# Turning queries and keys once, and swapping their halves by transfers inside SBUF, in a two-layer hybrid transformer block

## The chip, the cores and the metric

The kernel runs on one core of a Trainium2 chip. Five engines work beside one another, each with an instruction queue of its own that it takes in order: TensorE (PE: matmuls, and transposes, which are matmuls with an identity), VectorE (DVE), ScalarE (ACT), GpSimdE (POOL), and SyncE (SP), which here issues the transfers (DMA). Semaphores order them against one another. The metric is device time in microseconds (us), the median of several runs.

## What is computed

Two layers work on 512 latent tokens and 256 context tokens of width 1024, with heads of 64 elements. Layer 0 has two parallel groups of attention heads, windowed ones with a sink and dense ones, four query heads to a key head; layer 1 has differential attention, two score maps per head. Queries and keys are normed and rotated, and then:

```python
# layer 0, dense heads (the windowed ones add a mask and a sink)
s = jnp.einsum('bqhgd,bkhd->bhgqk', qb, k).astype(jnp.float32) * scale
p = _softmax(s, sink_b).astype(v.dtype)
return jnp.einsum('bhgqk,bkhd->bqhgd', p, v)
...
# layer 1
s = jnp.einsum('bqhad,bkhad->bhaqk', qb, k).astype(jnp.float32) * scale
p = jax.nn.softmax(s, axis=-1)
a = (p[:, :, 0] - lam * p[:, :, 1]).astype(v.dtype)
return jnp.einsum('bhqk,bkhe->bqhe', a, v)
```

Each layer ends in an output projection and a SwiGLU feed-forward block. Everything is in float32.

## The kernel before, in words

**Split operands.** Matmuls run on a reduced float32 format (F32R). An operand is split into a high part (the value rounded to that format, a ScalarE copy) and a low part (the value less the high part, a subtraction), and products are summed from the parts. A head has only 64 elements, so a score matmul, whose contraction takes 128 partitions, holds both parts of an operand at once: one part in partitions 0 to 63, the other in 64 to 127. All four products of parts are wanted: high by high, low by low, and the two crossed ones. So each score takes two matmuls into one accumulator.

**How the four products are made before.** In layer 0 the query is turned (transposed by TensorE into its working layout) as high above low. The key is turned twice: once as high above high, once as low above low. The first matmul gives both query parts times the key's high part, the second both times its low part. In layer 1 it is the other way round: the key is turned as high above low, and the query twice, as high above high and as low above low.

**Layer 0, from 60 to 385 us.** `in_proj0` (lines 505 to 546) projects one group of heads b (four query heads, one key, one value head) for six tiles of 128 tokens, context tiles 4 and 5 first, then 0 to 3. For each tile it empties the accumulator (`qkv`, line 520), norms and rotates (`rotate`), multiplies by the norm's factor (line 523), splits the queries (`qd`, lines 524 to 526) and the key (`kd`, 527 to 530; the key stands doubled in it), and puts two calls on a list: `turn_q` (four transposes into a PSUM tile `qpt`, one ScalarE copy of 512 columns into `qt`) and `turn_k` (two transposes into `kpt`, one copy of 256 columns into two rows of `kT`). `attend0` (from line 548) takes one tile of queries through scores (lines 573 to 581, four heads with two matmuls per stretch of keys), softmax, transposes of the probabilities (`ppt`) and the product with the values (`av`). While group b attends, group b + 1 is projected and turned between its steps. The last tile of each group is turned early in the next group's attention, but all that is left is turned before group 3 starts (line 1320): group 3 begins with a tile that needs all keys.

**Layer 1, from 975 to 1300 us.** `Proj1` projects head h for the six tiles. `finish` (lines 672 to 689) empties the accumulator `inps`, rotates and splits; its `transposes` (691 to 703), called some steps later from the list `late`, turns queries (four transposes into `qpt`, one copy of 512 columns into `qt`) and keys (two transposes into `kpt`, one copy of 256 columns into `kT`). Context tiles have no queries, so 32 of 48 calls turn queries. `attend1` (from line 706) makes the scores of one head and one query tile, two softmaxes, their difference, and the product with the values. The main loop (from line 1673) runs three half-tiles of projection beside each attention step, so projection is about a head and a half ahead.

**Weights.** Layer 1's weights come in units of two 128-row blocks: three SP loads into one of two raw buffers (line 365), a ScalarE cast to the high part (line 370), a GpSimdE subtraction to the low part (line 371, `wil`). A load waits until its raw buffer is free, and everything behind it on SP waits too. In layer 0 SP loads projection weights (line 491), modulation weights `modw` (line 177, 512 KB each, in the same raw buffers) and, near 301 us, the output projection's weights (line 771).

**What sets the order.** TensorE's order is that of the code, written by hand, in most of the kernel (`tc.manual_schedule` on PE: from line 1175 to 1214, and from the sixth attention step of layer 0 to the end). Layer 0's projection of group 0 and its first attention steps lie outside. The order on all other engines, SP among them, comes from a planner that goes by priorities (program order, mostly) and by its own estimate of when an instruction can start. Semaphores follow from the order.

Of the kernel before, what the change touches and what calls it, by code (L numbers as in the profile page):

```python
# [12 lines left out]
F32R = mybir.dt.float32r  # L13
# [6 lines left out]
P = 128  # L20
# [7 lines left out]
HD = 64  # L28
# [23 lines left out]
def bc(ap, pos, n):  # L52

    dims = [list(d) for d in ap.ap]
    return AP(ap.tensor, ap.offset, dims[:pos] + [[0, n]] + dims[pos:])
# [8 lines left out]
def backbone(es: ExitStack, tc: tile.TileContext, x, c, ctx, c_ctx, mod_w, mod_b, norm_mix_w, norm_ffn_w,  # L64
# [3 lines left out]
    nc = tc.nc  # L68
# [47 lines left out]
    def f32(ap):  # L116
        return ap.bitcast(F32)
# [383 lines left out]

    def tables0(j, tabs, wp):
        tabs[j] = rope_tables(wp, *((ev_qn_a[0], ev_kn_a[0]) if j == 0 else (ev_qn_b[0], ev_kn_b[0])))

    def in_proj0(b, ws, tabs, wp, st, later, begun={}):
# [5 lines left out]
        for t in CTX_FIRST:  # L511
# [15 lines left out]
            kd = wp.tile([P, 2, 2, HD], F32R, name="kd", tag="kd", bufs=2)  # L527
            kb = bc(y[:, 4, :], 1, 2)
            nc.scalar.copy(kd[:, 0], kb)
            nc.gpsimd.tensor_sub(kd[:, 1], kb, f32(kd[:, 0]))  # L530
# [9 lines left out]
            def turn_k(t=t, kd=kd):  # L540
                pk = tr_tile("kpt", [P, 2, P], F32R)
                for j in range(2):
                    nc.tensor.transpose(pk[:, j, :], kd[:, j].rearrange("p a d -> p (a d)"), identr)
                nc.scalar.copy(kT[:, :, t * P:(t + 1) * P], f32(pk))
# [3 lines left out]
    def attend0(b, t, state, o_t, sink, negsink, mp):  # L548

        qs, kT, vv = state  # L550
# [14 lines left out]
        if isA and nx and t < NTX - 1:  # L565
            masks.append((t + 1 - xt0, 1))
        P4 = mp.tile([P, 4, TOK], F32, name="Pt", tag="Pt", bufs=2)
# [89 lines left out]
    class Proj1:  # L657
# [14 lines left out]
        def finish(self, t, ps):  # L672
# [9 lines left out]
            if nq:  # L682
                qd = wp.tile([P, 2, 2, 2, HD], F32R, name="qd", tag="qd", bufs=3)
                yb = bc(y[:, 0:2], 2, 2)
                nc.scalar.copy(qd[:, 0], yb)
                nc.vector.tensor_sub(qd[:, 1], yb, f32(qd[:, 0]))
# [4 lines left out]
            def transposes():  # L691
                if nq:
                    pt = tr_tile("qpt", [P, 2, 2, P], F32R)
                    for j in range(2):
                        for a in range(2):
                            nc.tensor.transpose(pt[:, j, a, :], qd[:, j, a].rearrange("p a d -> p (a d)"), identr)
                    qt = self.qp.tile([P, 2, 2, P], F32R, name="qt", tag="qt", bufs=5)
                    nc.scalar.copy(qt, f32(pt))
                    qs[t] = qt
# [6 lines left out]
    def attend1(h, t, state, o_t, nlam, subln, mp):  # L706
# [3 lines left out]
        E = []  # L710
        for a in range(2):
# [1219 lines left out]
```

## Time and profile before

| | |
|---|---|
| median of 3 runs | 1695.23 us (1695.23 to 1698.65) |
| span of the profiled execution | 1695.6 us; no other time is given for it |
| granted TensorE clock | 0.992 |
| VectorE, ScalarE, GpSimdE busy | 1146.7, 937.0, 696.4 us |
| transposes that turn queries | 96 in layer 0, 128 in layer 1 |
| transposes that turn keys | 48 in layer 0, 96 in layer 1 |
| transfers issued by SP and ACT | 194.64 MB at a mean of 115 GB/s |

A row of the groups names the line, the engine, the operation, the tile written and those read, the shape and the count; behind the bar stands the time in which at least one of the group was running, then the mean length of one in ns; behind the second bar the idle time ahead of them and who ended it. A row of the waits gives the total in us, the number and the longest. A row of the timeline gives start and length in us. A row of the transfers gives their size and the median time from issue to landing.

### The profile page before, as it was taken

To read this page: it belongs to the slowest core of one execution; us is meant where nothing else is said; L and a number is where in the kernel's file an instruction comes from. 1 tells how busy PE (TensorE), PEld (TensorE's weight loads), DVE (VectorE), ACT (ScalarE), POOL (GpSimd) and SP (SyncE) were. 2 spreads that over 40 slices of the span, in tenths; PEclk is the share of its full clock that TensorE was granted. 3 is DMA by queue.
4 is the path that set the end of the run, shared out by engine and by line. 5 is a ranking of instruction groups with operands and counts; after the bars stand their busy time and mean duration, and the time that the engine had idled before them with its cause. 6 is when DMAs were issued, how large, how long until landed. Compare 5 with 4: busy or idle time off the path is not lost. (4 is left out here: it accounts for less than half of the span.)

```text
span 1695.6 us, 28585 instructions
## 1 busy us (share of the span) xinstructions
PE 1631.5 (96%) x10390; PEld 1468.6 (87%) x10390; DVE 1146.7 (68%) x2014; ACT 937.0 (55%) x2011; POOL 696.4 (41%) x867
## 2 busy tenths in 40 slices
PE   6999999899999999999999989999999999999998
PEld 3977787677999999998777889999988899999887
DVE  3765656754799887767767656666666598887434
ACT  5565555745456665545554456666666555555320
POOL 2665554321346554412413366666664242221000
PEclk8999999999999999999999999999999999999999
DMA  9222221411455555439966311111112433331431
GB/s 319 69 71 74 70 70 50 164 60 38 129 167 172 164 159 162 134 108 347 296 184 189 99 43 38 48 42 44 50 45 97 125 93 102 111 101 57 137 99 62
DMA packets 218108, 194.64 MB, mean 115 GB/s; under 512 B 20016, under 2 KB 202864, under 8 KB 217968
## 3 DMA queue, kind: packets, MB, share of 16 engines
q1 hardware_dynamic: 217616, 192.62, 36.8%
q8 instruction: 81, 1.33, 0.3%
q14 instruction: 59, 0.48, 0.1%
q10 hardware_dynamic: 352, 0.21, 0.0%
HBM read 179.92 MB, written 12.87 MB: 114 GB/s over the span
## 5 line engine op out<-in xcount | busy, mean ns | idle before, releaser
L901 ACT CAST wbh<-wr 128x512 fp32r<-128x512 f32 x170 | 104.9, 621 | 130.2 <-PE p L933 73.4
L933 PE MATMUL p<-hT,wbh 128*128 128x256 f32 (+1 forms) x752 | 154.5, 299 | 0.0
L465 PE MATMUL inps<-wih,hT 128*128 128x384 f32 x512 | 144.2, 344 | 7.3 <-ACT qkv L677 7.3
L911 POOL TENSOR_TENSOR wbl<-wr,wbh 128x512 fp32r<-128x512 f32 x43 | 60.0, 1396 | 173.6 <-ACT wbh L901 173.6
L933 PEld LDWEIGHTS p<-hT,wbh 128*128 128x128 f32 x752 | 121.9, 191 | 0.2
L911 DVE TENSOR_TENSOR wbl<-wr,wbh 128x512 fp32r<-128x512 f32 x127 | 107.7, 858 | 21.0 <-ACT wbh L901 16.8
L933 PE MATMUL p<-hT,wbl 128*128 128x256 f32 (+1 forms) x376 | 111.9, 298 | 0.0
L933 PE MATMUL p<-t,wbh 128*128 128x384 f32 (+1 forms) x480 | 111.3, 318 | 0.0
L604 POOL TENSOR_SCALAR Pt<-Pt,rc 128x256 f32<-128x256 f32 (+3 forms) x96 | 74.6, 788 | 89.3 <-DVE rc L601 83.1
L231 POOL TENSOR_TENSOR modp<-modp 128x512 f32<-128x512 f32 x40 | 57.4, 1436 | 114.3 <-ACT modp L230 114.3
L465 PEld LDWEIGHTS inps<-wih,hT 128*128 128x128 f32 x512 | 93.3, 188 | 10.6 <-ACT qkv L677 9.7
L933 PE MATMUL p<-hTt,wbh 128*128 128x256 f32 (+1 forms) x480 | 101.0, 302 | 0.0
L887 POOL TENSOR_TENSOR wr<-wr 128x512 f32<-128x512 f32 x40 | 61.6, 1540 | 89.8 <-DVE ws L892 85.8
L933 PE MATMUL p<-b,wbh 128*128 128x384 f32 x368 | 93.8, 336 | 0.2 <-DVE c L961 0.2
L901 ACT CAST wbh<-ws 128x512 fp32r<-128x512 f32 x120 | 69.4, 579 | 43.1 <-PE p L933 29.0
L224 DVE SCALAR_TENSOR_TENSOR ma<-modw,cols,ma 128x256 f32<-128x256 f32 x140 | 89.2, 637 | 2.3
L592 ACT ACTIVATE Pt<-sc,nm 128x256 f32<-128x256 f32 (+3 forms) x96 | 67.6, 707 | 35.3 <-DVE nm L588 16.9
L465 PE MATMUL inps<-wil,hT 128*128 128x384 f32 x256 | 86.0, 336 | 0.0
L933 PEld LDWEIGHTS p<-t,wbh 128*128 128x128 f32 x480 | 82.9, 189 | 0.0
L911 DVE TENSOR_TENSOR wbl<-ws,wbh 128x512 fp32r<-128x512 f32 x120 | 81.7, 681 | 1.7 <-ACT wbh L901 1.6
L933 PEld LDWEIGHTS p<-hTt,wbh 128*128 128x128 f32 x480 | 78.3, 191 | 3.1 <-ACT modp L230 1.6
L230 ACT ACTIVATE modp<-modw,cols 128x256 f32<-128x256 f32 x160 | 68.4, 500 | 18.0 <-POOL ma L236 10.1
(355 smaller groups left out, 5217.9 us busy)
## 6 DMA issues: line engine op xcount, KB each, us to landing
modw<-in_mod_w_dram SPq DMA_DIRECT2D x96, 512.0 KB, 5.2
wr<-in_ffn_w_in_dram SPq DMA_DIRECT2D x176, 256.0 KB, 2.9
wdr<-in_ffn_w_out_dram SPq DMA_DIRECT2D x66, 512.0 KB, 3.7
wir<-in_od_w_in_dram SPq DMA_DIRECT2D x96, 128.0 KB, 2.3
hidm<-hid SPq DMA_DIRECT2D x44, 192.0 KB, 1.9
hr<-hidm SPq DMA_DIRECT2D x22, 192.0 KB, 3.5
x<-in_x_dram SPq DMA_DIRECT2D x8, 512.0 KB, 3.5
wir<-in_ev_w_in_dram SPq DMA_DIRECT2D x16, 256.0 KB, 3.5
```

What stands on the lines that cost most here:

```text
L224: nc.vector.scalar_tensor_tensor(acc, w[:, k], scale[k], acc, ALU.mult, ALU.add)
L230: nc.scalar.activation(pr[:, k], w[:, k], AF.Copy, scale=scale[k])
L231: nc.gpsimd.tensor_add(pr[:, 0:2], pr[:, 0:2], pr[:, 2:4])
L465: nc.tensor.matmul(ps, hs[j][:, k, :], ws[k // 2][z][:, k % 2, c0:c1], start=(k, j, z) == (0, 0, 0), stop=(k, j, z) == (KT - 1, 1, 0))
L592: turn["exp"] = nc.scalar.activation(p[:, :n], s, AF.Exp, bias=nm[:, c1], accum_out=sm[:, c1])
L604: nc.gpsimd.tensor_scalar(p[:, :n], p[:, :n], rc[:, hh:hh + 1], 1.0, ALU.mult, ALU.mult)
L887: nc.gpsimd.tensor_sub(w, raw[f, "G1"], w)
L901: nc.scalar.copy(hi, w)
L911: (nc.gpsimd if name == "G2" else nc.vector).tensor_sub(lo, raw[need[n]], f32(hi))
L933: nc.tensor.matmul(ps, w[:, k, :], H[b][h][:, k, :], start=first and k == 0 and q == 0, stop=final and k == 3 and q == 2, skip_group_check ...
```

## The change

Each operand that was turned twice is now turned once, as high above low. A second copy with the halves exchanged, low above high, is made from it by two transfers from SBUF to SBUF, one for each half of the partitions, issued by SP. Scores then come from (high above low) by (high above low) and (high above low) by (low above high); the four products are the same.

In layer 0 this concerns the keys (24 tiles: four groups, six tiles): one transpose and not two, a copy of 128 columns and not 256, and a split of 64 columns and not 128. Each transfer moves 64 partitions of 512 bytes. In layer 1 it concerns the queries (32 tiles: eight heads, four tiles): two transposes and not four, a copy of 256 columns and not 512, and a split of 128 columns and not 256 on ScalarE and on VectorE. Each transfer moves 64 partitions of 1024 bytes. Scores have as many matmuls as before.

`halves_swapped` puts a swap on a list and issues all but the newest; the newest is issued with the next one or, by `swapped()`, when the next attention step is begun in the code. In the code's order each swap so stands ahead of the scores that read it.

```diff
@@ -499,6 +499,18 @@
+    swaps = []
+
+    def swapped(left=0):
+        while len(swaps) > left:
+            to, src = swaps.pop(0)
+            for j in range(2):
+                nc.sync.dma_start(f32(to[HD * (1 - j):HD * (2 - j)]), f32(src[HD * j:HD * (j + 1)]))
+
+    def halves_swapped(to, src):
+        swaps.append((to, src))
+        swapped(1)
+
@@ -524,10 +536,9 @@
-            kd = wp.tile([P, 2, 2, HD], F32R, name="kd", tag="kd", bufs=2)
-            kb = bc(y[:, 4, :], 1, 2)
-            nc.scalar.copy(kd[:, 0], kb)
-            nc.gpsimd.tensor_sub(kd[:, 1], kb, f32(kd[:, 0]))
+            kd = wp.tile([P, 2, HD], F32R, name="kd", tag="kd", bufs=2)
+            nc.scalar.copy(kd[:, 0], y[:, 4])
+            nc.gpsimd.tensor_sub(kd[:, 1], y[:, 4], f32(kd[:, 0]))
@@ -538,10 +549,11 @@
-                pk = tr_tile("kpt", [P, 2, P], F32R)
-                for j in range(2):
-                    nc.tensor.transpose(pk[:, j, :], kd[:, j].rearrange("p a d -> p (a d)"), identr)
-                nc.scalar.copy(kT[:, :, t * P:(t + 1) * P], f32(pk))
+                pk = tr_tile("kpt", [P, P], F32R)
+                nc.tensor.transpose(pk, kd.rearrange("p a d -> p (a d)"), identr)
+                cs = slice(t * P, (t + 1) * P)
+                nc.scalar.copy(kT[:, 0, cs], f32(pk))
+                halves_swapped(kT[:, 1, cs], kT[:, 0, cs])
@@ -564,6 +576,7 @@
+        swapped()
         P4 = mp.tile([P, 4, TOK], F32, name="Pt", tag="Pt", bufs=2)
@@ -680,22 +693,21 @@
-                qd = wp.tile([P, 2, 2, 2, HD], F32R, name="qd", tag="qd", bufs=3)
-                yb = bc(y[:, 0:2], 2, 2)
-                nc.scalar.copy(qd[:, 0], yb)
-                nc.vector.tensor_sub(qd[:, 1], yb, f32(qd[:, 0]))
+                qd = wp.tile([P, 2, 2, HD], F32R, name="qd", tag="qd", bufs=3)
+                nc.scalar.copy(qd[:, :, 0, :], y[:, 0:2])
+                nc.vector.tensor_sub(qd[:, :, 1, :], y[:, 0:2], f32(qd[:, :, 0, :]))
...
-                    pt = tr_tile("qpt", [P, 2, 2, P], F32R)
-                    for j in range(2):
-                        for a in range(2):
-                            nc.tensor.transpose(pt[:, j, a, :], qd[:, j, a].rearrange("p a d -> p (a d)"), identr)
+                    pt = tr_tile("qpt", [P, 2, P], F32R)
+                    for a in range(2):
+                        nc.tensor.transpose(pt[:, a, :], qd[:, a].rearrange("p a d -> p (a d)"), identr)
                     qt = self.qp.tile([P, 2, 2, P], F32R, name="qt", tag="qt", bufs=5)
-                    nc.scalar.copy(qt, f32(pt))
+                    nc.scalar.copy(qt[:, 0], f32(pt))
+                    halves_swapped(qt[:, 1], qt[:, 0])
                     qs[t] = qt
@@ -708,6 +720,7 @@
+        swapped()
         for a in range(2):
             sc = p_sc.pool.tile([P, 1024], F32, name="sc", tag="sc", bufs=2)
```

## The prediction

> **What bounds the kernel now.** I read the page's totals first, then a table of two stretches, then the groups of instructions, then the waits, the transfers, and the timeline around the places that the change touches.
>
> ```profile
> PE 1631.5 (96%) x10390; PEld 1468.6 (87%) x10390; DVE 1146.7 (68%) x2014; ACT 937.0 (55%) x2011; POOL 696.4 (41%) x867
> ```
>
> TensorE is busy for 96% of the span and no other engine for more than 68%. An average over stages proves little, so the second view cuts out the two stretches that hold every edited line: layer 0's attention (60 to 385 us) and layer 1's (975 to 1300 us). Columns: length, then busy time per engine with its instructions, the granted clock, the share of the transfer engines, GB/s.
>
> ```profile
> 60.00:385.00 325.00, 304.30 (x2166) 246.45 (x2165) 201.66 (x459) 192.34 (x478) 162.18 (x248) 0.99 0.24 78
> 975.00:1300.00 325.00, 308.72 (x2133) 292.72 (x2132) 207.46 (x413) 212.09 (x539) 214.94 (x340) 0.99 0.18 51
> ```
>
> TensorE is the bound in both: 304.3 and 308.7 of 325 us, the others at most 215. Its clock is 0.99, so nothing is to be had there. What TensorE no longer does comes off the end, unless a new wait takes its place; its idle time, 20.7 and 16.3 us, is all that a lighter ScalarE or GpSimdE could give beyond that.
>
> **The change part by part.** Layer 1's queries: 32 tiles go from four transposes to two. Layer 0's keys: 24 tiles go from two to one. The groups (all of the run; busy time is after the bar, then the mean of one in ns):
>
> ```profile
> L696 PE MATMUL qpt<-identr,qd 128*128 128x128 f32 x128 | 16.9, 254 | 0.9 <-ACT qt L698 0.8
> ...
> L702 PE MATMUL kpt<-identr,kd 128*128 128x128 f32 x96 | 16.0, 249 | 1.7 <-POOL kd L689 1.6
> ...
> L535 PE MATMUL qpt<-identr,qd 128*128 128x128 f32 x96 | 11.7, 245 | 0.8 <-ACT qt L537 0.6
> ...
> L543 PE MATMUL kpt<-identr,kd 128*128 128x128 f32 x48 | 7.6, 237 | 0.7 <-ACT kT L544 0.6
> ```
>
> The mean is useless here, since transposes overlap; the busy time of a group of four against a group of two tells what two more cost. Layer 1: 16.9/32 = 528 ns against 16.0/48 = 333 ns, so two are worth 195 ns, and 32 tiles 6.2 us. Layer 0: 11.7/24 = 488 against 7.6/24 = 317, so one is worth 85 ns, and 24 tiles 2.0 us. The busy time holds part of the last transpose's tail, which doesn't go with the count; I take 5.6 and 2.0, together 7.6 us off TensorE's path, between 8.2 and, with as much taken off once more, 7.0.
>
> The evictions and splits shrink with them:
>
> ```profile
> L698 ACT CAST qt<-qpt 128x512 fp32r<-128x512 f32 x32 | 18.7, 586 | 2.7 <-PE qpt L696 2.6
> ...
> L703 ACT CAST kT<-kpt 128x256 fp32r<-128x256 f32 x48 | 18.2, 378 | 1.2 <-PE kpt L702 1.2
> ...
> L688 ACT CAST kd<-qy 128x128 fp32r<-128x128 f32 x48 | 14.3, 299 | 15.0 <-POOL qy L680 14.8
> ...
> L685 ACT CAST qd<-qy 128x256 fp32r<-128x256 f32 x32 | 13.0, 406 | 23.4 <-POOL qy L680 23.4
> ```
>
> In layer 1 each qt copy goes from the 512-wide row to the size of the 256-wide one (586 to 378 ns) and each qd cast from the 256-wide to the 128-wide (406 to 299): 0.31 us of ScalarE per tile, 10 us in all, beside TensorE's work. VectorE's qd difference, and in layer 0 the kd pair and the kT copy, shrink on engines that are idle over a third of the time; I cost them at nothing, and TensorE's busy stream is what hides them. Does ScalarE's relief reach TensorE? TensorE's largest wait in the second stretch is this (us in total, times, longest):
>
> ```profile
> PE inps L465 <- ACT qkv L677: 7.7, 10, 1.4
> ```
>
> That wait is the accumulator being emptied. Where a transpose group stood between the last projection and the next, it covered part of it, and that cover gets thinner by 0.17 us: 10 waits could grow by 1.7 us. A ScalarE with 5% less to do could shorten them by about as much, or by 2 us at best. I take 0.5 us of gain, between -2 and +1.7.
>
> What is added: two transfers within SBUF per tile, 112 in all, all issued by SP. No transfer of this kind is in the trace. The nearest rows, with the time from issue to landing, and SP's time for one issue (min/median/max):
>
> ```profile
> modw<-in_mod_w_dram SPq DMA_DIRECT2D x96, 512.0 KB, 5.2
> ...
> wir<-in_od_w_in_dram SPq DMA_DIRECT2D x96, 128.0 KB, 2.3
> ...
> out_dram<-x SPq DMA_DIRECT2D x2, 128.0 KB, 1.7
> L365 SPq DMA_DIRECT2D wir<-in_od_w_in_dram x42: 367/469/1345, 1020.0 to 1143.7; - x42
> ```
>
> A transfer of 32 KB (keys) or 64 KB (queries) should land some 1.7 to 2.3 us after its issue, if nothing is ahead of it; a pair takes SP about 0.9 us. So a swapped operand is there 2.6 to 3.2 us after its copy. Where its reader comes later than that, it costs nothing. [...]
>
> Layer 1's lead is long. Timeline, start and duration:
>
> ```profile
> 1019.67 0.59 ACT L698 CAST qt<-qpt 128x512 fp32r<-128x512 f32 x1
> 1029.41 0.59 ACT L698 CAST qt<-qpt 128x512 fp32r<-128x512 f32 x1
> 1040.53 0.35 PE L715 MATMUL sc<-kT,qt 128*128 128x256 f32 x1
> 1040.72 0.28 PE L716 MATMUL sc<-kT,qt 128*128 128x256 f32 x1
> 1040.84 0.40 PE L715 MATMUL sc<-kT,qt 128*128 128x512 f32 x1
> 1041.08 0.39 PE L716 MATMUL sc<-kT,qt 128*128 128x512 f32 x1
> 1059.59 0.37 SPq L365 DMA_DIRECT2D wir<-in_od_w_in_dram  x1
> 1061.97 0.35 PE L715 MATMUL sc<-kT,qt 128*128 128x256 f32 x1
> ```
>
> The query tile copied at 1019.67 is used at 1040.53, the one of 1029.41 at 1061.97: 20 us and more, against 3.2 needed. Behind a swap that waits for its copy, SP has only the weight loads of the next head; the code holds one swap back, so that its copy is mostly done when it is issued. A load that is held up by one pair is late by 0.9 us; the loads that a projection needs soon come two groups a head, so 7 heads could lose up to 7 x 0.9 = 6 us if nothing else covered it. I take 0.3, since the weight split of a load issued at 1020 is used several us later; the range keeps 0 to 6. The wait that each first use of a swapped tile adds to TensorE is one more among waits that the scores carry already; the score group that begins here waits for a bank and two operands and its matmuls still follow one another at the pace of the stream:
>
> ```profile
> 1111.07 0.28 PE L715 MATMUL sc<-kT,qt 128*128 128x256 f32 x1
> 1111.19 0.28 PE L716 MATMUL sc<-kT,qt 128*128 128x256 f32 x1
> ```
>
> 0.12 us apart, so 56 such waits cost 0 to 0.08 us each (0.08 is what the pair at 1040.53, 0.19 apart, takes more): 0.2 us taken, 4.5 at most.
>
> Layer 0 has one exposed place. The last head group's first scores, at 300 us, read all keys right after the last of them was turned:
>
> ```profile
> 299.20 0.33 PE L543 MATMUL kpt<-identr,kd 128*128 128x128 f32 x2
> 299.88 0.38 ACT L544 CAST kT<-kpt 128x256 fp32r<-128x256 f32 x1
> 300.16 0.92 SPq L177 DMA_DIRECT2D modw<-in_mod_w_dram  x2
> 300.46 0.98 PE L578 MATMUL sc<-kT,qt 128*128 128x256 f32 x4
> 301.13 0.49 SPq L771 DMA_DIRECT2D wor<-in_ev_w_out_dram  x1
> ```
>
> The four score matmuls are spaced like the four at 1040.53 (0.19, 0.12, 0.24 us), so the one that reads the swapped half of the last key tile starts at 300.46 + 0.55 = 301.0. The copy ends at 300.26. At best the pair is issued at once: 300.26 + 0.9 + 1.9 = 303.1, a stall of 2.1 us. At worst it goes out after the two 512 KB modw loads and lands behind them: 301.1 + 0.9 + 5.2 = 307.2, a stall of 6.2. Behind the stalled matmul stands everything that TensorE has, as its order is written by hand there; VectorE's row maximum, and through it ScalarE, wait for it. I take 3.5, nearer the lower end, since SP may well send the pair between the two loads. The first scores of all follow their key copy as closely:
>
> ```profile
> 76.77 0.36 ACT L544 CAST kT<-kpt 128x256 fp32r<-128x256 f32 x1
> 77.39 0.70 PE L578 MATMUL sc<-kT,qt 128*128 128x256 f32 x4
> 77.94 0.33 PE L465 MATMUL inps<-wihi,hTc 128*128 128x384 f32 x1
> ```
>
> There the planner orders TensorE and has projections to put ahead, as the third line shows; I take 0.5 us, between 0 and 2.6.
>
> **Sum.** -5.6 - 2.0 - 0.5 + 0.3 + 0.2 + 3.5 + 0.5 = -3.6 us. The profiled execution's span is 1695.6 us, 0.4 above the median of 1695.2, so the forecast of 1692.0 for such a span is 1691.6 as a median.
>
> **The rivals.** First, the saving is given back in layer 0: the pair at 300 us lands behind both modw loads (+6.2 instead of 3.5), and the thinner cover in front of the accumulator's emptying costs 1.7 instead of gaining 0.5. That gives 1691.6 + 2.7 + 2.2 = 1696.5 at its worst, 1694.5 with half. For it: the loads' issue at 300.16 is earlier than the copy's end, and every transfer of SP goes through one queue. [...] Against it: SP's order comes from a planner that sees the pair as ready before the second load.
>
> Second, slower: swaps stand on SP behind a weight load that is being held. SP's own waits show the hold (us in total, times, longest):
>
> ```profile
> SPq L365 <- POOL rs_q L159: 162.0, 7, 29.4
> ```
>
> Seven times, once a head, SP stands at a load until a raw buffer is free; the load at 1059.59 ends one. If the swap of the third query tile (copied at 1029.41) were queued behind such a load, it would go out after that unit's three issues, at 1059.59 + 3 x 0.47 = 1061.0, and land at 1061.0 + 0.9 + 2.3 = 1064.2. Its matmul would start, 0.19 after 1061.97, at 1062.2: 2.0 us of stall, 14 us over seven heads, 1705. It decides as soon as the pair is issued later than 1059; before the hold it has 30 us. Earlier tiles can't be behind it, as the load itself waits for work that follows their scores. Against it: the copy is done 30 us before the hold ends.
>
> Third, more gain: the pair at 300 us goes out at once (stall 2.1), ScalarE's relief gives its 2 us: 1691.6 - 1.4 - 1.5 = 1688.7.
>
> **How the numbers follow.** A measurement of this kernel can tell about 0.2%, 3.4 us, from no change: faster means below 1691.8, slower above 1698.6. The forecast case has 0.48 (1689 to 1694; its middle lies at the border: 0.28 below, 0.20 within), the first rival 0.24 (0.18 within, 0.06 slower, if held-up loads and first-use waits come to their upper ends as well), the held swaps 0.12 (slower), more gain 0.16 (faster). So faster 0.44, same 0.38, slower 0.18. The forecast's own range is 1689 to 1694; for eight in ten it reaches down to the third rival with the larger transpose saving, 1685, and up through the first rival to 1700, which leaves out the held swaps and little else.
>
> **What would show it.** In the profile after: L696's successor with 64 and L543's with 24 transposes, qt copies near 380 ns; TensorE's busy time in the second stretch lower by 5 to 6 us and in the first by 2; one idle gap of 2 to 6 us ahead of the scores near 300 us, released by a transfer; no TensorE wait for a transfer in layer 1. The prediction is wrong if scores of layer 1 wait for swapped queries, if weight splits release projections more often than now, or if TensorE's idle time in the second stretch grows by as much as its busy time falls.

## The result, and the profile after

The changed kernel takes 1708.9 us (median of 6 runs, 1707.8 to 1710.7) beside 1695.2 us for the kernel before (6 runs beside them): a ratio of 1.0080, 95% interval 1.0068 to 1.0091. It is slower by 13.6 us, and outside the range of 1685 to 1700. The profiled execution's span is 1707.5 us, 11.9 above that of before, and it is this difference that is placed below. In every run that has both, the time is 1.7 to 2.1 us above the span, so the profiled execution of before stands for some 1697.4 us, 2 us above its median: the traces show somewhat less of the loss than the medians do.

The edit did on the engines what it says. First the page's totals after, then three groups of instructions (columns: the count, min/median/max in ns, first and last start in us), then the two kinds of transfer it added (size, median us from issue to landing).

```profile
PE 1629.1 (95%) x10302; PEld 1462.9 (86%) x10302; DVE 1149.9 (67%) x2014; ACT 923.9 (54%) x2011; POOL 694.6 (41%) x867
```

```profile
L707 PE MATMUL qpt<-identr,qd x64: 222/231/305, 997.0 to 1280.8; 128*128 128x128 f32 x64
L709 ACT CAST qt<-qpt x32: 364/367/380, 998.4 to 1281.1; 128x256 fp32r<-128x256 f32 x32
...
L553 PE MATMUL kpt<-identr,kd x24: 220/221/281, 68.3 to 301.8; 128*128 128x128 f32 x24
```

```profile
qt<-qt SPq DMA_DIRECT2D x64, 64.0 KB, 2.7
kT<-kT SPq DMA_DIRECT2D x48, 32.0 KB, 1.9
```

There are 88 transposes fewer, the copies are as short as forecast (367 ns for 378), and the key transfers land in 1.9 us, within the 1.7 to 2.3 us that were taken; the query transfers took 2.7 us, above them (few landings are recorded, seven of 64 here). The two stretches of the prediction, after (length, busy time by engine, clock, transfer share, GB/s):

```profile
60.00:385.00 325.00, 297.93 (x2091) 239.60 (x2090) 195.94 (x447) 182.37 (x463) 155.16 (x240) 0.98 0.26 80
975.00:1300.00 325.00, 301.18 (x2045) 285.85 (x2046) 211.98 (x408) 196.75 (x531) 215.81 (x341) 0.99 0.23 65
```

TensorE is busy for 6.4 and 7.5 us less in 325 us. Part of that is only that the work comes later: the stretches lack 75 and 88 matmuls where 24 and 64 transposes were taken out. Over the whole span TensorE's busy time falls by 2.4 us and its idle time grows by 14.3, from 64.1 to 78.4. Matching the same matmuls in both traces tells where. The start of a matmul after, minus its start before:

| place | after minus before | in this stage |
|---|---|---|
| 122 us, start of layer 0's attention | +5.9 | +5.9 |
| 290 us, end of the third head group | +2.8 | -3.1 |
| 311 us, layer 0's fourth head group has begun | +8.5 | +5.7 |
| 975 us, end of layer 0's feed-forward | +9.0 | +0.5 |
| end | +11.9 | +2.9 |

Three stages lose clearly and one gains. The gain, and the sizes of the first and the last loss, are not what the sum had. The first 62 us, which hold no edited line, came out 1.4 us shorter after, so the edited part of the first stage lost 7.3 us. Counted so, the stages add up to 13.3, near the 13.6 of the medians. One pair of traces is a rough measure, though: in six other traces the edited lines lie behind 840 us, and they reach that point between 2.4 us ahead of this execution of before and 0.3 behind it.

**Around 300 us.** First TensorE's longest wait for a transfer, then stretches of 3 us, before and after.

```profile
PE sc L591 <- DMA kT<-kT: 3.3, 1, 3.3
```

```profile
304.00:307.00 3.00, 2.50 (x18) 1.93 (x17) 2.55 (x5) 2.42 (x6) 0.78 (x1) 1.00 1.00 345
307.00:310.00 3.00, 3.00 (x29) 1.73 (x26) 1.22 (x3) 1.48 (x4) 2.24 (x4) 1.00 1.01 396
```

```profile
304.00:307.00 3.00, 0.03 (x1) 0.06 (x1) 0.00 (x0) 0.00 (x0) 0.00 (x0) 0.80 0.82 250
307.00:310.00 3.00, 3.00 (x14) 2.90 (x15) 1.19 (x3) 0.63 (x2) 0.00 (x0) 0.50 1.03 392
310.00:313.00 3.00, 3.00 (x15) 2.70 (x15) 1.65 (x2) 1.49 (x4) 0.00 (x0) 0.56 1.03 421
```

Before, no stretch is idle. After, the scores wait 3.3 us for the last key tile's swap; then the granted clock is 0.50 for 6.8 us, and 14 matmuls go where 29 went. The wait costs 3.1 us and the low clock 2.6.

**In layer 1.** TensorE's waits for a weight's low part, between 975 and 1300 us, before and then after:

```profile
PE inps L465 <- POOL wil L371: 1.0, 1, 1.0
```

```profile
PE inps L465 <- POOL wil L371: 7.6, 6, 1.5
PE inps L465 <- ACT qkv L690: 7.5, 12, 1.5
```

The second line of after was 7.7 before: ScalarE's relief changed nothing there. The first grew by 6.6 us. The same place in one head, SP's timeline and then GpSimdE's and ScalarE's, before:

```profile
1019.99 3.60 SPq L365 DMA_DIRECT2D wir<-in_od_w_in_dram  x6
```

```profile
1020.32 1.84 POOL L371 TENSOR_TENSOR wil<-wir,wih 128x768 fp32r<-128x768 f32 x1
1024.98 1.84 POOL L371 TENSOR_TENSOR wil<-wir,wih 128x768 fp32r<-128x768 f32 x1
```

and after:

```profile
1028.63 0.38 SPq L365 DMA_DIRECT2D wir<-in_od_w_in_dram  x1
1029.10 1.11 SPq L508 DMA_DIRECT2D qt<-qt  x2
1030.26 1.11 SPq L365 DMA_DIRECT2D wir<-in_od_w_in_dram  x2
1031.47 1.11 SPq L508 DMA_DIRECT2D qt<-qt  x2
1032.68 1.58 SPq L365 DMA_DIRECT2D wir<-in_od_w_in_dram  x3
```

```profile
1033.67 0.83 ACT L370 CAST wih<-wir 128x768 fp32r<-128x768 f32 x1 [1.87 <-DMA wir<-in_od_w_in_dram]
```

```profile
1034.58 1.82 POOL L371 TENSOR_TENSOR wil<-wir,wih 128x768 fp32r<-128x768 f32 x1 [0.91 <-ACT wih L370]
```

A unit of a weight is three loads. Before, the third unit's loads go out as soon as its buffer is free (1019.99), and its low part is done 6.8 us later, just when TensorE needs it (1026.8). After, the buffer is free at 1028.6, but a pair stands between the first load and the other two, so that the unit is complete 1.1 us later and its low part is ready 7.8 us after the buffer, at 1036.4. TensorE had stood idle for 1.4 us by then.

### The profile page after: what moved, and what is told of

It reads as the page before. It is cut to its first block, busy times and chain, and to the rows that moved or that the text cites. A ratio compares the mean times of both kernels' runs of the same rounds, so it can differ in the third digit from the quotient of the medians.

```text
span 1707.5 us, 28652 instructions
## 1 busy us (share of the span) xinstructions
PE 1629.1 (95%) x10302; PEld 1462.9 (86%) x10302; DVE 1149.9 (67%) x2014; ACT 923.9 (54%) x2011; POOL 694.6 (41%) x867
```

## The experiments

The theory: the loss has three places (the start of layer 0's attention, the hand-over at 300 us, the swap pairs between layer 1's loads), and each can be mended by itself. The rivals: the planner's new order as a whole, or transposes that are worth nothing. Ratios are to the kernel before, run beside each kernel. A head of layer 1 is the time between the first projection matmuls of successive heads in the trace, the median of six. Head groups of layer 0 are counted from 1.

| kernel | ratio, 95% interval | median us | head, us |
|---|---|---|---|
| before | | 1693.1 to 1695.2 | 39.7 |
| after | 1.0080 (1.0068 to 1.0091) | 1708.9 | 40.0 |
| keys only | 1.0068 (1.0053 to 1.0083) | 1706.1 | 39.75 |
| queries only | 1.0032 (1.0018 to 1.0046) | 1698.9 | 39.9 |
| all, ScalarE's queue | 1.0233 (1.0215 to 1.0250) | 1734.3 | 44.0 |
| all, queries behind loads | 1.0091 (1.0074 to 1.0109) | 1709.0 | 40.1 |
| keys, group 1 | 1.0035 (1.0022 to 1.0047) | 1700.2 | |
| keys, groups 2 and 3 | 0.9986 (0.9975 to 0.9996) | 1692.0 | |
| keys, group 4 | 1.0023 (1.0012 to 1.0033) | 1698.9 | |
| group 4, wait filled | 1.0041 (1.0027 to 1.0054) | 1700.6 | |
| group 1, x tiles only | 1.0019 (1.0009 to 1.0030) | 1698.0 | |
| group 1, no transfer | 0.9998 (0.9987 to 1.0009) | 1695.1 | |
| queries, loads first | 0.9994 (0.9981 to 1.0007) | 1693.3 | 39.15 |
| queries, no transfer | 1.0014 (1.0005 to 1.0023) | 1695.5 | 39.8 |
| queries, no transfer, loads first | 1.0016 (1.0007 to 1.0024) | 1697.5 | 39.8 |
| before, loads first | 1.0009 (0.9998 to 1.0020) | 1696.9 | 39.7 |
| queries, loads first, exp ahead | 1.0022 (1.0012 to 1.0033) | 1698.5 | 40.0 |
| all, loads first | 1.0062 (1.0048 to 1.0077) | 1706.0 | 39.1 |
| combined | 0.9984 (0.9973 to 0.9995) | 1691.3 | 39.2 |
| combined, queries as before | 1.0003 (0.9993 to 1.0012) | 1694.6 | 39.75 |

**Each half by itself.** Keys only: layer 1 as before.

```diff
-                    pt = tr_tile("qpt", [P, 2, P], F32R)
...
+                    pt = tr_tile("qpt", [P, 2, 2, P], F32R)
...
-                    halves_swapped(qt[:, 1], qt[:, 0])
```

> Layer 0's keys are swapped by transfers as in the changed kernel; layer 1's queries are turned twice on TensorE as before. Theory (three places each lose something: the start of layer 0's attention, the last score tile before 300 us with the clock after it, and layer 1's weight groups held up on SP): the loss of layer 0 stays whole and layer 1 gives back nothing and loses nothing, so the span is 8 to 9 us above the kernel before, some 1703 to 1705, with a TensorE wait of about 3 us for a transfer into kT near 300 us. Rival (the order that the planner wrote down has changed throughout, and the loss is in no one place): the span lies anywhere from 1692 to 1709 and the wait near 300 us need not be there.

Measured: 11.5 us above before, more than expected. In the traces the same matmuls are late by 6.7 us at 120 us, by 4.2 at 200 and by 8.9 after 305, and layer 1's heads take what they took before. Queries only: layer 0 as before.

```diff
-                pk = tr_tile("kpt", [P, P], F32R)
...
-                halves_swapped(kT[:, 1, cs], kT[:, 0, cs])
+                pk = tr_tile("kpt", [P, 2, P], F32R)
```

> Layer 1's queries are swapped by transfers; layer 0's keys are turned twice on TensorE as before. Theory (the swap pairs stand on SP between the weight loads that a projection needs): up to 975 us every matmul stands where it stood before, and each head of layer 1 waits 1.0 to 1.5 us for a weight split, which eats the 0.7 us of its transposes: 2 to 4 us above the kernel before, 1697 to 1699. Rival (layer 1's loss in the changed kernel came from the shift that layer 0 handed on to it, not from the swaps): no waits for weight splits beyond those of before, and about 5.5 us below it, 1690.

Measured: 5.4 us above before, with 7.0 us of waits for low parts. So layer 1 loses without anything handed on from layer 0; that rival is out. The halves add to 16.9 us, the whole change is 13.6; the intervals allow that difference.

**Another queue, another place.** The swaps from ScalarE's queue:

```diff
-                nc.sync.dma_start(f32(to[...]), f32(src[...]))
+                nc.scalar.dma_start(f32(to[...]), f32(src[...]))
```

> The whole change, with the swaps issued from ScalarE's queue and not from SP's. Theory (SP's order is what costs): the waits of TensorE for weight splits in layer 1 go back to what they were before, and layer 1 ends 4 to 6 us earlier relative to its start than before; the transfer that the scores near 300 us wait for no longer stands behind a held weight load on SP, so that wait is at most 3 us as it was or shorter. ScalarE issues 112 transfers more, at about half a microsecond each, 56 us beside 924 busy. In sum 1697 to 1703. Rival (layer 1 loses because every transfer beside the loads slows them, whatever queue issues it): the waits for weight splits stay at 1.0 to 1.5 us a head and the time stays at 1707 to 1711.

TensorE's waits in layer 1 with the swaps on ScalarE's queue:

```profile
PE inps L465 <- POOL wil L371: 16.3, 6, 2.7
PE inps L465 <- ACT qkv L690: 10.4, 15, 1.4
```

The expectation fell: 39 us above before, the waits for low parts twice as long. Each of the six waits is of 2.7 us, one a head, and after each the granted clock is 0.50 for 3.4 us. ScalarE makes the high part from which the low part comes, and a transfer issued there takes 0.47 us of its own queue. In one head the third unit's cast starts 0.5 us later than in the changed kernel (1034.18 against 1033.67), behind an exponential, and its subtraction 1.7 us later (1036.31 against 1034.58), behind a step of a norm on GpSimdE. So the order on both engines is another one; which of it the issues on ScalarE's queue bring about is not shown. Next, the pairs on SP behind the last load written ahead of them:

```diff
+            with behind("load"):
+                for j in range(2):
+                    nc.sync.dma_start(...)
```

> The whole change, with each of layer 1's swap pairs put behind the weight loads that were written down ahead of it on SP, and layer 0 left as changed. Theory (the pairs between the loads are what makes layer 1 lose): the waits for weight splits shrink to those of before, layer 1 gains 3 to 6 us over the changed kernel, 1703 to 1706. If the pairs then come too late, the scores of layer 1 wait for swapped queries instead. Rival (contention of the transfers, not their place on SP): the waits stay and the time stays at 1707 to 1711.

Nothing moved: SP's order in layer 1 is the same as in the changed kernel, since the loads in question were already ahead in the code and SP's planner put the pair between later ones. It decides nothing. What does separate them is a precedence for a unit's loads:

```diff
-        for dst, src in views(raw):
-            turn["load"] = nc.sync.dma_start(dst, src)
+        with tc.high_priority(300):
+            for dst, src in views(raw):
+                turn["load"] = nc.sync.dma_start(dst, src)
```

> Layer 1's queries are swapped by transfers and layer 0 is as before, but the three loads of a weight group have precedence on SP over a swap pair, so that no pair stands between them (six loads, a pair, three loads, a pair, three loads in a head). Theory (the pair between the loads of the third group is what makes TensorE wait 0.9 us a head): those waits go and the transposes' 5 us are gained, 1688 to 1691. Rival (the waits come of DMA engines shared with the swaps, or layer 1 is bound elsewhere): the waits stay, 1697 to 1700.

The same two waits with the loads kept together:

```profile
PE inps L466 <- ACT qkv L691: 6.6, 10, 1.5
PE inps L466 <- POOL wil L372: 3.2, 6, 1.0
```

The waits fall from 7.0 to 3.2 us and a head from 39.9 to 39.15; the time is 1.0 us below before (interval from 3.2 below to 1.2 above), 6.4 us below queries only by the ratios. In the traces the part from 975 us on is 2.7 us shorter than before's; in nine other kernels with before's layer 1 it lies between 1.8 us shorter and 1.3 longer. The place between the loads is shown to be the cause of layer 1's loss; half a microsecond a head is left of the wait.

The precedence seems to have a price of its own. In all seven kernels with it SP issues six of layer 1's loads ahead of a load of layer 0's feed-forward weights near 905 us, where before issued five. In six of the seven TensorE then waits 1.1 to 1.2 us for that weight's low part, and in none of the other kernels; the seventh (combined, queries as before) has the order without the wait, so the cause isn't shown.

**Layer 0 by head group.** The three kernels differ in one line (`b` counts the groups from 0):

```diff
+    ONCE = (0,)    # or (1, 2), or (3,)
...
+            if b in ONCE:
+                kd = wp.tile([P, 2, HD], F32R, name="kd", tag="kd", bufs=2)
```

> Of the whole change only the keys of layer 0's first head group are swapped by transfers; all other keys and layer 1's queries are turned twice on TensorE as before. Theory (the stretch from 60 to 123 us, where no order was written down by hand, loses because each score there needs a transfer that lies between the last key's emptying and the scores): the loss of that stretch, 5 to 8 us, appears whole, and nothing is lost near 300 us: 1698 to 1702. Rival (it is the second group's keys, which are projected in the same stretch, or no one group): within 2 us of the kernel before.

> Only the keys of layer 0's second and third head groups are swapped by transfers; the rest is as before. Theory (these swaps land long before their scores are due): 12 transposes fewer at 0.08 us each, so between 2 us below and 1 us above the kernel before, 1692 to 1695. Rival (the second group's swaps disturb the stretch up to 123 us): 4 to 8 us above it.

> Only the keys of layer 0's fourth head group are swapped by transfers; the rest is as before. Theory (the last pair is late by 3 us at 300 us, and the clock falls after the idle time, for 2.6 us more): nothing changes up to 300 us, then 4 to 6 us are lost at once and kept: 1698 to 1701. Rival (the wait comes of the delay that the earlier groups handed on): the last pair is in time and the kernel is within 1 us of the one before.

Measured: 5.9 us above, 2.4 below and 3.9 above before: the theory and not the rival in all three cases, though groups 2 and 3 gain more than the 1.0 us that 12 transposes at 0.08 us make, and group 4 loses a little less than expected. Together they make 7.4 us, where the keys as a whole cost 11.5; the intervals just meet, and group 2 is projected in the stretch in which group 1 loses. TensorE's waits at the start, for the first group alone, and then its stretches of 6 us from 84 us, before and with the first group's keys swapped:

```profile
PE ppt L638 <- POOL Pt L630: 2.6, 1, 2.6
PE sc L604 <- ACT Pt L618: 2.4, 2, 2.1
```

```profile
84.00:90.00 6.00, 5.79 (x36) 5.41 (x36) 2.73 (x11) 3.30 (x13) 5.82 (x12) 1.00 0.05 12
90.00:96.00 6.00, 4.97 (x44) 3.00 (x43) 5.44 (x20) 4.81 (x17) 4.11 (x9) 1.00 0.52 177
```

```profile
84.00:90.00 6.00, 3.44 (x30) 2.89 (x33) 3.97 (x15) 3.61 (x13) 3.29 (x6) 1.00 0.09 22
90.00:96.00 6.00, 5.75 (x30) 4.86 (x23) 1.82 (x9) 1.70 (x7) 4.69 (x11) 0.50 0.56 177
```

No wait there is for a transfer. The last two of the first tile's four score products start at 85.7 us where before they started at 82.6, since the planner, which orders this stretch, spread them out; the weights they make are late, TensorE runs out of projections and stands idle for 2.6 us, and then the clock is 0.50 for 6.8 us. Two kernels ask why the order changed: the swap left to the four x tiles, and no transfer at all.

```diff
-            if b in ONCE:
+            if b == 0 and t < NTX:
```

> Only the first head group's keys are swapped, and of these only the four tiles of x; the two context tiles, whose keys the first scores need, are turned twice as before. Theory (the start loses because the first score tiles, which use the context keys alone, need a transfer, and the planner spreads them out): the scores near 77 and 83 us stand as before, the idle time of 2.6 us near 87 us goes, and the time is within 2 us of the kernel before. Rival (any edit of the first group upsets the order of this stretch): 3 to 7 us above it.

```diff
-                    halves_swapped(kT[:, 1, cs], kT[:, 0, cs])
...
-                        nc.tensor.matmul(..., q, kT[:, j, c0:c1], ...)
+                        nc.tensor.matmul(..., q, kT[:, j if b else 0, c0:c1], ...)
```

> The first head group's keys of layer 0 turned once and no transfer made: that group's scores use the unswapped keys twice, so the cross products of its scores are left out. All else is as before. Theory (the start loses because the planner puts the first scores later, having a transfer ahead of them): the idle time of 2.6 us near 87 us and the low clock after it go, within 1.5 us of the kernel before. Rival (any edit of these instructions gives another order that loses): 3 to 7 us above it.

Without transfers the loss is gone (0.9998; 1.6 us of idle time are left at 89 us, and no low clock follows), so it is the transfers, as the planner reckons with them, and not the fewer transposes. With the swap in the x tiles only, the idle time near 87 us and the low clock are gone and the matmuls at 131 us start 0.7 us earlier than before; yet the ratio is 1.0019, some 3 us above before. The 2.3 us by which its profiled execution is longer all arise after 900 us, in code that the edit doesn't touch; 1.7 of them come between 1260 and 1280 us, where the clock is low for 6.8 us and in before's execution for 3.4. That tells of one execution; why the eight runs lie 3 us above before stays open.

The wait at 300 us filled with work that nobody reads:

```diff
             if t == 0:
+                warm = tr_tile("warm", [P, 4, P])
+                for k in range(22):
+                    nc.tensor.transpose(warm[:, k % 4, :], cst[:, :P], ident)
                 scores0(i)
```

> The fourth group's keys are swapped as in the run of that group alone, and 22 transposes of a constant, about 2.9 us of added work whose result nobody reads, stand on TensorE ahead of the scores that wait near 300 us. Theory (the fall of the granted clock follows from TensorE being idle for 3 us): the wait is filled, so the scores start as late as they did, within 0.5 us, but the clock stays at 1.00 and 1 to 2 us less are lost by 320 us than in the run of that group alone. Rival (the clock falls for another reason, such as the transfers that start there): the clock falls at the same place and the loss is the same or larger.

Stretches of 3 us, with group 4 alone and then with the wait filled:

```profile
301.00:304.00 3.00, 0.99 (x5) 0.95 (x6) 0.41 (x1) 0.00 (x0) 0.00 (x0) 0.89 0.95 288
304.00:307.00 3.00, 3.00 (x14) 2.81 (x15) 1.47 (x4) 1.48 (x3) 0.00 (x0) 0.54 1.01 393
```

```profile
301.00:304.00 3.00, 2.38 (x20) 2.05 (x19) 0.00 (x0) 0.00 (x0) 0.00 (x0) 1.00 0.90 280
304.00:307.00 3.00, 3.00 (x26) 2.82 (x26) 2.54 (x5) 1.77 (x4) 0.00 (x0) 1.00 1.04 391
```

The transfers are the same, the clock stays at 1.00, and from the late score to 307 us the kernel makes up 1.6 us on the one with the idle wait. So it is the idle time that takes the clock down here; each kernel was traced once, and the five other traces with a wait of 3.2 us or more near 300 us all have the low clock behind it. The whole time doesn't show that gain (1.0041 beside 1.0023, intervals overlapping).

**What a transpose of layer 1 is worth.** No transfer, and both products from the unswapped operand:

```diff
-                    halves_swapped(qt[:, 1], qt[:, 0])
...
-                nc.tensor.matmul(so, qs[t][:, 1, a, :], kT[:, a, k0:k1], start=False, stop=True)
+                nc.tensor.matmul(so, qs[t][:, 0, a, :], kT[:, a, k0:k1], start=False, stop=True)
```

> Layer 1's queries are turned once and no transfer is made at all: both products of a score use the unswapped operand, so the cross products of high and low parts are left out of layer 1's scores. Layer 0 is as before. Theory (the transposes are worth their 5 us, and what takes it back is on SP): the waits for weight splits are those of before and the time is 4 to 6 us below the kernel before, 1688 to 1690. Rival (layer 1 is held by something else, so that fewer transposes gain nothing): within 2 us of the kernel before, 1692 to 1696.

The theory failed here. The query transposes' busy time falls from 2.11 to 1.36 us a head (from a group's start to the next matmul's, it is 1.73 and 1.15), the waits for low parts are small (2.8 us), and a head takes 39.8 us as before. So either 0.6 to 0.75 us a head is worth nothing, or something else came in. Two kernels cross the precedence of the loads (the edit above) with the kernel before and with this one:

> The kernel before with the one edit that gives a weight group's three loads precedence on SP; every transpose is as before and nothing is swapped. Theory (the waits for weight splits that the swaps brought are the only thing this edit mends): before has nearly none of these waits, so it stays within 1.5 us of the kernel before and a head of layer 1 takes 39.7 us as it did. Rival (the edit itself is what shortened the heads to 39.15 us, and the queries turned once gained nothing): about 39.2 us a head, 3 to 4 us below the kernel before.

> Layer 1's queries turned once, no transfer made (both products of a score use the unswapped operand, so the cross products are left out), and a weight group's loads have precedence on SP. Theory (fewer transposes are worth up to 0.78 us a head once the weight splits keep up): 39.0 us a head, 1688 to 1691. Rival (with 0.78 us less on TensorE a head meets the emptying of its accumulator by ScalarE and the weight splits instead, as in the run without transfers): 39.7 us a head, 1693 to 1696.

Before stays at 39.7 us a head, and without transfers it stays at 39.8. The precedence by itself does nothing, and the shorter heads need something that the kernel without transfers lacks. ScalarE's timeline in one head, with the swaps and the loads first, shows it:

```profile
1070.33 0.90 ACT L734 ACTIVATE e<-sc,mx 128x768 f32<-128x768 f32 x1 [0.58 <-DVE mx L732]
...
1071.44 0.37 ACT L691 COPY qkv<-inps 128x256 f32<-128x256 f32 x1
1071.71 0.91 ACT L734 ACTIVATE e<-sc,mx 128x768 f32<-128x768 f32 x1
```

One exponential, the emptying of an accumulator, the other exponential. Before has this order too. In the kernels without transfers both exponentials come first; the same place without transfers:

```profile
1069.80 0.90 ACT L732 ACTIVATE e<-sc,mx 128x768 f32<-128x768 f32 x1
...
1070.69 0.90 ACT L732 ACTIVATE e<-sc,mx 128x768 f32<-128x768 f32 x1
...
1071.57 0.37 ACT L690 COPY qkv<-inps 128x256 f32<-128x256 f32 x1
```

There the emptying is 0.6 us later in the head, and TensorE's waits for it are 0.80 us a head and not 0.34. To try this order, the emptying goes behind the last exponential:

```diff
-            nc.scalar.copy(raw[:, :n], ps[:, :n])
+            with behind("exp"):
+                nc.scalar.copy(raw[:, :n], ps[:, :n])
```

> The kernel with layer 1's queries swapped and the loads kept together, with one thing changed: ScalarE's emptying of a projection's accumulator is put behind the last exponential written ahead of it, which in each head moves one exponential of about 0.9 us (and nothing on TensorE or SP) from behind an emptying to ahead of it, the order that ScalarE has in the runs without a transfer. Theory (the 0.6 us a head that those runs lost is this inversion on ScalarE): a head goes from 39.15 to about 39.75 us and the kernel is 3 to 5 us slower than with the loads kept together, 1696 to 1698. Rival (the heads without transfers were long for another reason): 39.15 us a head, within 1.5 us of the loads kept together.

The same place of the head, with that edit:

```profile
1071.70 0.90 ACT L735 ACTIVATE e<-sc,mx 128x768 f32<-128x768 f32 x1 [0.60 <-DVE mx L733]
...
1072.77 0.90 ACT L735 ACTIVATE e<-sc,mx 128x768 f32<-128x768 f32 x1
...
1073.66 0.36 ACT L692 COPY qkv<-inps 128x256 f32<-128x256 f32 x1
```

A head goes from 39.15 to 40.0 us and the kernel from 0.9994 to 1.0022; the waits for the emptying are 0.97 us a head. TensorE's and SP's orders are the same. The planner also moved, in each head, a copy of the probabilities on ScalarE and one step of a rotation on VectorE, so the inversion is not quite alone. The transposes are worth 0.56 us a head (39.71 to 39.15) as long as ScalarE keeps its order; this inversion is enough to take all of it. The kernels without transfers differ from the one with the loads first in more places on ScalarE, VectorE and GpSimdE; that it is all they lose by is not shown.

**Together.** The keys of groups 2 and 3 and of group 4 without its last tile, the queries, and the loads first:

```diff
+            if b in (1, 2) or b == 3 and t != CTX_FIRST[-1]:
                 kd = wp.tile([P, 2, HD], F32R, name="kd", tag="kd", bufs=2)
```

> Layer 0's keys are swapped by transfers in the second and third head groups and in the fourth but for its last key tile; the first group and that tile are turned twice as before. Layer 1's queries are swapped by transfers, with a weight group's three loads kept together ahead of a pair on SP. Theory (the losses have places of their own, and these are left out): the gains of the two parts add up, 2.6 and 1.3 us, and there is no wait for a key transfer near 300 us: 1689 to 1692, faster than both kernels. Rival (any other order moves the start or the hand-over by itself): 1694 or more.

> Layer 0's keys as in the combined version (second and third group, and the fourth but for its last key tile); layer 1's queries turned twice as before, with the precedence of the loads. Theory (the queries turned once are worth some 0.6 us a head): 2 to 4 us slower than the combined version, 1692 to 1695. Rival (they are worth nothing): within 1 us of the combined version, 1690 to 1692.

> The whole change with one line more, the precedence of a weight group's loads on SP. Theory (of the changed kernel's loss the pairs between the loads are 0.8 to 0.9 us a head, the rest is layer 0's): the waits for weight splits fall from 1.0 to 0.5 us a head or less, a head takes 39.2 us, and the kernel is 4 to 6 us below the changed one, 1703 to 1705, still slower than before. Rival (in the whole change the heads are long by what layer 0 hands on): within 2 us of the changed kernel.

The combined kernel is at 0.9984, 2.7 us below before and, by the ratios, 16 below the changed kernel; its clock stays at 1.00 around 300 us, with no wait for a transfer there. With the queries as before it loses 3.2 us of this and its heads take 39.75 us: a second measurement of what the queries are worth. The whole change with the loads first gains 3.0 us on the changed kernel (ratios 1.0080 and 1.0062, the intervals just overlap), less than the 4 to 6 expected. Its heads are short, and from 975 us on its trace is 5.7 us shorter than the changed kernel's; but it loses 4.7 us between 900 and 940 us, in layer 0's feed-forward, where the precedence seems to have its price and the clock falls once more. The rest is layer 0's attention, with a wait of 2.8 us and a low clock near 200 us that the changed kernel's profiled execution didn't have.

## Why the prediction was wrong

The bound was named rightly. What is saved was named about rightly as busy time: 0.75 us of TensorE a head, 0.70 in the sum. From a group's start to the next matmul's it is 0.58, and with the loads kept together the queries turned once were worth 2.5 us beside before with the loads first and 3.2 us in the combined kernel, not the sum's 5.6. These steps failed.

- **"I take 0.3, since the weight split of a load issued at 1020 is used several us later"** is the step that turned the sign in layer 1. The load is used 6.8 us later, but all of these are taken: landing, ScalarE's cast (0.84), GpSimdE's subtraction (1.84), with no slack at the end. One pair in front is 1.1 us in TensorE's wait. The term measured 6.6 us, a little above the end of 6 that the text gave it, and ate the transposes' 5.6.
- **+0.5 for the first scores** was 7.3 us, counted from 62 us (5.9 by the runs of group 1 alone). The text took TensorE's free order there as protection. It was the opening: with a transfer ahead of the scores the planner wrote another order, and its idle time (2.6 us) brought the low clock (0.50 for 6.8 us).
- **+3.5 at 300 us** was 5.7. The wait is as forecast (3.3 us; one 512 KB load went ahead of the pair, as assumed). What the text didn't have is the clock after an idle time (0.50 for 6.8 us here, 2.6 us of the loss): "nothing is to be had there" reads a mean of 0.99 as if it couldn't fall.
- **-2.0 for layer 0's transposes** came out as a gain of 3.1 us between 122 and 290 us, most of it from a place that the prediction didn't look at. TensorE's wait there, before and with only groups 2 and 3 swapped:

```profile
PE ppt L612 <- ACT qt L537: 2.9, 1, 2.9
```

```profile
PE ppt L638 <- ACT qt L555: 1.4, 1, 1.4
```

The first ends at 198 us with a clock of 0.50 for 3.4 us behind it; the second leaves the clock at 1.00. Not all of it is the edit's: of the seven traced kernels that have before's layer 0 this wait was between 1.97 and 2.93 us, and the clock fell in four. Nor does it come of these groups' transposes alone. With only group 1 swapped, and groups 2 and 3 turned as before, the same wait is short and the same stretch gains 2.9 us:

```profile
PE ppt L638 <- ACT qt L555: 1.5, 1, 1.5
```

The transposes' own share is smaller than the term: the keys' busy time on TensorE fell from 7.6 to 5.6 us as in the sum, but from start to next start only from 5.0 to 3.7. What shortens the wait stays open.

- **-0.5 for ScalarE's relief** was nothing. For the +0.2 of first uses, no wait of a score in layer 1 for a transfer shows.

Of the rivals, the pair behind the loads at 300 us went with one load ahead, between the forecast and the rival. The held swaps didn't happen, so that their 1705 lies nearer to the measured time than the forecast does is luck. The reverse did: SP stood at swaps until ScalarE had made the copies of that tile, with loads behind them.

```profile
SPq L508 <- ACT kT L555: 75.3, 12, 10.5
SPq L508 <- ACT kT L715: 52.3, 15, 6.4
```

The prediction took the one swap that the code holds back for a guard against this; the planner, which sets SP's order, doesn't keep the code's order. The two transfers of a pair, one for each half of the partitions, overlapped at 32 KB: the second of a key pair was issued 0.5 us after the first and landed 1.9 us after its issue, the first 1.8 (medians of the landings recorded, six of 24 each). Of the three signs named for a wrong prediction one came true in full: weight splits release projections more often. The third, idle time in the second stretch that grows by what its busy time falls, says nothing as it was worded, since in a stretch of fixed length it always does. With the same work on both sides (975 to 1300 us before, 984.1 to 1311.9 after) TensorE's busy time falls by 4.2 us and its idle time grows by 7.0. Two slips in the prediction's figures carry no weight: half of the first rival's 4.9 us gives 1694.05 and not 1694.5, and the third rival with the larger transpose saving gives 1688.1, so the lower end of 1685 is not worked out from its terms.

## What to carry to other kernels

Before a transfer is put on a queue that also carries loads, follow the load behind it to its last user: a chain without slack turns each issue ahead of it into waiting time (here 1.1 us for a pair, 6.6 us in layer 1), however early the load seems to go out. Look in the same way at a precedence that mends it, which puts those loads ahead of others. Work taken off the bounding engine counted here only as long as ScalarE kept its order (a head of 39.15 us, and of 40.0 with the order changed), so compare the order on each engine before and after, not the busy times alone. Price an idle time of TensorE with the low clock that may follow it: in these traces 26 of the 38 of 2.1 us and more brought it.

## What the runs showed of the hardware

That the clock falls within a kernel whose mean is 0.99 was not expected. All idle times of TensorE over 1.2 us between 55 and 1690 us in the twenty traces, and whether the granted clock went to 0.50 after them:

| idle time | low clock after it |
|---|---|
| 3.1 us and more | 6 of 6 |
| 2.4 to 3.1 us | 18 of 25 |
| 2.1 to 2.2 us | 2 of 7 |

Shorter ones brought it mostly near 1266 us, where several follow one another (in before one of 1.4 us, with the clock at 0.50 for 3.4 us after it). The low clock starts 2 to 5 us after the idle time began and lasts 3.4 or 6.8 us in the traces' clock records. The length alone doesn't decide: 20 of 32 idle times of 2.1 to 3.1 us brought the low clock and 12 didn't, and what parts them is not shown. One fall cost 1.6 us where it was taken away (the filled wait) and 2.6 us around 300 us, so two executions of one kernel can differ by that. In 115 runs of the kernel before the time goes with the granted clock: the 18 with a clock of 0.993 or less took 1697.1 us in the mean, the 14 with 0.997 or more 1692.7. How much of that spread (1690.9 to 1700.9 us in one set of runs) the falls make, and which of the two brings the other, no run separates.
